# A hybrid attention layer on one core: branch B without normalised rows, output-weight sums by accumulating DMAs, weight scales finished on GpSimd

## The chip, the cores and the metric

The kernel runs on one core of a Trainium2 chip. The metric is the time of one execution on the device, in microseconds (us); smaller is better. The engines are TensorE (PE), VectorE (DVE), ScalarE (ACT), GpSimd (POOL) and SyncE (SP), which here only issues DMAs.

## What is computed

One layer on 512 tokens of width 2048, with 16 learned tokens ahead of them (528 keys). A single input projection feeds two branches. Cut to what matters:

```
proj = rms_norm(h) @ w_in          # q_a, ckv, z_a, indexer q/k/w, q_b, k_b, v_b, z_b, g_a, g_b
# branch A, 8 heads: per query the top keys by an indexer's scores, softmax over them in a latent space
# branch B, 8 heads, queries and keys in two halves of 64:
attn = softmax(q1 k1 * s + bias) - lam * softmax(q2 k2 * s + bias)   # block-causal
o_b  = rms_norm(attn @ v_b, subln_w) * (1 - lam_init)
y_a, y_b = (o_a * silu(z_a)) @ w_o_a, (o_b * silu(z_b)) @ w_o_b
mix  = sigmoid(g_a) * y_a + sigmoid(g_b) * y_b
out  = h + rms_norm(mix @ w_out, post_norm_w)
```

Since o_b is normalised per row, a row of attn may be multiplied by any positive number, as long as the norm's epsilon is multiplied by its square.

## The kernel before

Every float32 factor is taken as a high and a low part of a shorter type, and a product is three passes of TensorE (high x high, high x low, low x high: `mm3`, lines 264 to 267). Weights of `w_in` come in units of 128 columns, two raw tiles of 512 KB each. A unit (class `Unit`) goes through four steps: SP loads its raw tiles (line 179); ScalarE sums the squares of each half (`squares`, line 117); GpSimd takes the maximum over all partitions (`over_rows`, an all-reduce, line 122); VectorE makes a power of two and its inverse from the maximum (`power_of_two`, lines 129 to 135); then ScalarE and VectorE split the raw tile by that scale into `hi` and `lo` (`split16`, lines 161 and 162). The code for a unit's steps stands ahead of the unit's use (`advance`): the loads come three units ahead, squares two, scale and split one. A scheduler then sets the order of all instructions on each engine when the kernel is built, by costs of its own; each engine works its list strictly in order.

The stages, by time: up to 80 us the norms and the first projections; to 186 the indexer's queries and scores; to 560 branch B, head by head; to 745 branch A's heads; to 845 the first gates; to 1230 the other gates in pairs of units (za, zb, then ga and gb; class `Pair`, lines 955 to 990, seven Strassen products per pair, and for zb two multiplications on GpSimd in `load_o`, line 1048); to 1394 the merge stage, 32 units of the two output projections `w_o` (24 products of 512 columns each), their scales made by `wo_bound` and `wo_split`; at last the product with `w_out`, again in seven Strassen products of which four need sums of quarters of `w_out`.

A head of branch B projects q, k and v (48 products each), and meanwhile the head before is attended, in small steps (`step`, `pending`), beside rounds of branch A's top-k (`run_topk`). `b_attend.blk` takes the scores of 128 queries, adds the bias and takes the maximum in one VectorE pass (`softmax`, line 643), combines and negates the maxima (647, 649), lets ScalarE exponentiate (651), then normalises: reciprocal of the two sums, times (1, -lam), one pass over the first probabilities (726) and one that adds the second (727). `pv_steps` transposes the result on TensorE (658). `kstack` writes high and low parts of the two key halves, each to both halves of the partitions (752, 753, 755), so that one product with stacked queries adds high and low.

The sums for `w_out` (`wt_load`, `wt_sums`, lines 250 to 262): 64 tiles of 256 KB are loaded by SP, VectorE subtracts them into 64 tiles, and DMAs from ScalarE's queue store these to `wout_t`; 14 of 16 groups in heads 1 to 7 of branch B, two in the merge stage.

Of the kernel before, what the change touches and what calls it, by code (L numbers as in the profile page):

```python
# [10 lines left out]
F32 = mybir.dt.float32  # L11
# [9 lines left out]
P = 128  # L21
# [47 lines left out]
def layer_kernel(ctx, tc, xt_d, xn_d, cols_d, w0_d, wi_d, wkv_d, wo_d, wout_d, lam_d, post_d,  # L69
# [11 lines left out]
    msq = nc.dram_tensor("o_sumsq", [NH, 512], F32, kind="Internal").ap()  # L81
    rsq = nc.dram_tensor("o_rstd", [NH, 512], F32, kind="Internal").ap()
# [17 lines left out]
    pscale = const.tile([P, 2], F32, name="pscale")  # L100
# [18 lines left out]
    def over_rows(ssq):  # L119

        r = wpool.tile([P, 16], F32, tag="rows", name="rows", bufs=4)[:, :ssq.shape[1]]
        nc.gpsimd.partition_all_reduce(r, ssq, P, bass_isa.ReduceOp.max)  # L122
        return r

    def power_of_two(r, exps):

        e = wpool.tile([P, 2], F32, tag="exp", name="exp", bufs=3)
        if r.shape[1] > 1:
            nc.vector.tensor_reduce(e[:, 0:1], r, AX.X, ALU.max)
            r = e[:, 0:1]  # L130
# [3 lines left out]
        nc.vector.tensor_scalar(sc[:, 0:1], t, -1.0, SFIELD * EXP1, op0=ALU.mult, op1=ALU.add)  # L134
        nc.vector.tensor_scalar(sc[:, 1:2], t, exps, None, op0=ALU.add)
# [110 lines left out]
    wt = {"next": 0, "loaded": []}  # L246

    def wt_load(pool, tags):
        k, n = divmod(wt["next"], 2)
        wt["next"] += 1  # L250
        t = []
        for tag, (ci, di) in zip(tags, ((0, 0), (0, 1), (1, 0), (1, 1))):
            t.append(pool.tile(HB, F32, tag=tag, name="wt"))
            d = nc.sync.dma_start(t[-1], wout_d[ci, di, k, :, 512 * n:512 * n + 512])
            tc.keep_in_program_order(d)
        wt["loaded"].append((k, n, t))
# [251 lines left out]
    nlam = pp.tile([P, 1], F32, name="nlam")  # L508
    nc.vector.tensor_sub(nlam, ldot[:, 1:2], ldot[:, 0:1])
    nc.vector.tensor_scalar(nlam, nlam, -LAM_INIT, None, op0=ALU.add)  # L510
    nc.vector.memset(pscale[:, 0:1], 1.0)
    nc.vector.tensor_copy(pscale[:, 1:2], nlam)
# [106 lines left out]

    PH = ap_.tile([P, 11, P], F32R, name="PH")  # L620
# [35 lines left out]
    def pv_steps(pr, VH, VL, VM, done):  # L656
# [32 lines left out]
        return [tr, pv]  # L689

    def b_attend(h, q, kk, vt):
        q1, q2 = q
        Vn = {}
        pr = p_tiles()
        g = bias_tile(NH + h)
# [759 lines left out]
```

## Time and profile before

| | us |
|---|---|
| median of 3 runs | 1561.2 (1558.08 to 1564.26) |
| the profiled execution: its time | 1558.4 |
| its span in the trace | 1556.6 |
| busy: TensorE | 1443.3 (93%) |
| busy: VectorE | 1161.6 (75%) |
| busy: ScalarE | 982.9 (63%) |
| busy: GpSimd | 150.3 (10%) |
| mean granted clock of TensorE, of 1 | 0.971 |

A busy share is a mean over stages with different limits, so a change is read in the stages that it touches: what the engine that is nearly always busy waits for there. Idle time marked "issue" is time in which an engine waited for nothing that the profile shows.

### The profile page before, as it was taken

What the parts mean: (1) busy time and instruction counts of PE and PEld (TensorE: products, weight loads), DVE (VectorE), ACT (ScalarE), POOL (GpSimd) and SP (SyncE); (2) the same over time, 40 slices, a digit from 0 to 9 for tenths busy, and PEclk for the clock granted to TensorE, in tenths of its full rate; (3) what the DMA queues carried; (4) which work ended last, traced back from release to release, by engine and by line L of the source; (5) the groups of instructions that cost most, each with busy time, mean ns of one, the idle gap of its engine ahead of it and who ended that gap; (6) DMA issues with size and microseconds to landing.
All of it is one profiled execution on the core that took longest, in us unless ns stands there. A gap on an engine that the chain in (4) does not pass through costs nothing. (4 is left out here: it accounts for less than half of the span.)

```text
span 1556.6 us, 25582 instructions
## 1 busy us (share of the span) xinstructions
PE 1443.3 (93%) x9474; PEld 1079.9 (69%) x9474; DVE 1161.6 (75%) x2328; ACT 982.9 (63%) x1749; POOL 150.3 (10%) x203
## 2 busy tenths in 40 slices
PE   7899998898988898999998889999999899999997
PEld 7688766766666666556587768888888544458885
DVE  7975888778888786565677777787778566566778
ACT  7364676656566676666676677777778544436555
POOL 3500000000000022212001100000000011000001
PEclk9899999999999999999999989999999999999999
DMA  6482365445545433122544534444445566446774
GB/s 208 147 272 77 123 203 163 151 141 190 196 140 193 136 116 118 53 96 69 186 155 154 162 116 136 137 141 135 135 144 166 186 211 205 147 167 225 240 248 147
DMA packets 98141, 246.70 MB, mean 158 GB/s; under 512 B 11144, under 2 KB 15432, under 8 KB 97888
## 3 DMA queue, kind: packets, MB, share of 16 engines
q1 hardware_dynamic: 81424, 215.44, 43.5%
q10 hardware_dynamic: 16592, 29.64, 5.1%
q8 instruction: 74, 1.21, 0.3%
q14 instruction: 51, 0.42, 0.1%
HBM read 203.01 MB, written 47.39 MB: 161 GB/s over the span
## 5 line engine op out<-in xcount | busy, mean ns | idle before, releaser
L969 PEld LDWEIGHTS <-wh 128*128 128x128 f16 x2464 | 243.5, 99 | 66.7 <-issue 25.0
L117 ACT ACTIVATE junk<-raw 128x1024 bf16<-128x1024 f32 x192 | 202.1, 1053 | 116.7 <-DMA raw<-in_wi_dram 84.9
L265 PE MATMUL acc<-u,hi 128*128 128x264 f16 (+1 forms) x832 | 267.6, 322 | 1.0 <-DVE kal L783 1.0
L266 PE MATMUL acc<-u,hi 128*128 128x264 f16 (+1 forms) x832 | 267.0, 321 | 0.0
L267 PE MATMUL acc<-u,lo 128*128 128x264 f16 (+1 forms) x832 | 267.0, 321 | 0.0
L969 PE MATMUL acc<-tu,wh 128*128 128x256 f16 x1408 | 237.3, 275 | 20.9 <-DVE r L978 16.1
L969 PE MATMUL acc<-tu,wl 128*128 128x256 f16 x704 | 193.5, 275 | 0.0
L969 PE MATMUL acc<-u,wh 128*128 128x256 f16 x1056 | 180.2, 277 | 9.9 <-ACT wh L161 9.9
L161 ACT ACTIVATE hi<-raw,scale 128x1024 f16<-128x1024 f32 x104 | 118.0, 1143 | 108.2 <-PE acc L266 106.2
L162 DVE SCALAR_TENSOR_TENSOR lo<-raw,scale,hi 128x1024 f16<-128x1024 f32 x104 | 132.9, 1283 | 41.9 <-ACT hi L161 41.2
L265 PEld LDWEIGHTS <-hi 128*128 128x128 f16 x1088 | 108.2, 99 | 79.8 <-issue 6.6
L267 PEld LDWEIGHTS <-lo 128*128 128x128 f16 x1088 | 108.0, 99 | 76.8 <-issue 1.9
L162 DVE SCALAR_TENSOR_TENSOR wl<-S,scale,wh 128x1024 f16<-128x1024 f32 x88 | 115.3, 1311 | 59.8 <-ACT wh L161 59.6
L266 PEld LDWEIGHTS <-hi 128*128 128x128 f16 x1088 | 108.1, 99 | 74.3 <-issue 2.1
L969 PE MATMUL acc<-u,wl 128*128 128x256 f16 x528 | 146.3, 277 | 3.5 <-DVE wl L162 3.5
L122 POOL PARTITION_ALL_REDUCE rows<-ssq x90 | 47.8, 531 | 974.9 <-ACT junk L117 880.6
L969 PEld LDWEIGHTS <-wl 128*128 128x128 f16 x1232 | 121.9, 99 | 20.1 <-DVE wl L162 4.8
L161 ACT ACTIVATE wh<-S,scale 128x1024 f16<-128x1024 f32 x88 | 100.2, 1140 | 33.5 <-DVE S L1076 33.5
L267 PE MATMUL acc<-og,lo 128*128 128x512 f16 x256 | 97.0, 379 | 0.0
L265 PE MATMUL acc<-og,hi 128*128 128x512 f16 x256 | 97.0, 379 | 0.0
L266 PE MATMUL acc<-og,hi 128*128 128x512 f16 x256 | 97.0, 379 | 0.0
L162 DVE SCALAR_TENSOR_TENSOR wl<-raw,scale,wh 128x1024 f16<-128x1024 f32 x66 | 85.4, 1294 | 14.1 <-ACT wh L161 14.0
(309 smaller groups left out, 2978.1 us busy)
## 6 DMA issues: line engine op xcount, KB each, us to landing
raw<-in_wi_dram SPq DMA_DIRECT2D x172, 512.0 KB, 4.3
wt<-in_wout_dram SPq DMA_DIRECT2D x64, 256.0 KB, 4.6
wout_t<-wt ACTq DMA_DIRECT2D x64, 256.0 KB, 3.1
raw<-in_wo_dram SPq DMA_DIRECT2D x32, 512.0 KB, 3.9
raw<-wout_t SPq DMA_DIRECT2D x32, 512.0 KB, 3.9
raw<-in_wout_dram SPq DMA_DIRECT2D x24, 512.0 KB, 4.8
sg<-r ACTq DMA_DIRECT2D x32, 256.0 KB, 3.3
sg<-sg SPq DMA_DIRECT2D x32, 256.0 KB, 3.0
```

The costliest lines, as they stand in the source:

```text
L117: nc.scalar.activation(j, src, AF.Square, accum_out=dst)
L122: nc.gpsimd.partition_all_reduce(r, ssq, P, bass_isa.ReduceOp.max)
L161: nc.scalar.activation(hi, src, AF.Copy, scale=s)
L162: nc.vector.scalar_tensor_tensor(lo, src, s, hi, op0=ALU.mult, op1=ALU.subtract)
L265: nc.tensor.matmul(out, aH, bH, start=start, stop=False)
L266: nc.tensor.matmul(out, aH, bL, start=False, stop=False)
L267: nc.tensor.matmul(out, aL, bH, start=False, stop=stop)
L969: nc.tensor.matmul(acc, a[:, k, :], b, start=first and k == 0 and x == 0, stop=last and x == 2, skip_group_check=True)
```

## The change

It has five parts.

1. Branch B's rows are not normalised: the first exponentials stay as they are, and the second ones are added with the factor -lam z1/z2. The sums z1 are kept in `Z1`, transposed and stored once (`put_sums`), and the norm of o_b adds P * eps * z1 squared in place of eps.
2. Low keys are made once: `kstack` writes one low tile for both halves and copies the high parts to the other half of the partitions by two DMAs of ScalarE's queue. The queries get a third and fourth tile with zeros in the other half (`qstack`, `QZ`), so that a product with the stacked low keys picks its half.
3. The bias pass works with -1 as its factor and takes the minimum of negated logits, the second pass starting from the first's result; lines 647 and 649 go.
4. The sums of `w_out` are made by DMAs that add to their destination, issued by GpSimd (`wt_chain`): 32 loads by SP, 64 accumulating DMAs, 64 stores by SP. The scheduler is no longer told to keep the loads' place. Two of the four sums have the other sign, which `mix_sums` and the second half of `post` take back.
5. A unit's squares are added over its columns by GpSimd ahead of the all-reduce (which then has one column), and the last two steps of `power_of_two` run on GpSimd.

The core of the diff:

```diff
     def over_rows(ssq):
 
-        r = wpool.tile([P, 16], F32, tag="rows", name="rows", bufs=4)[:, :ssq.shape[1]]
-        nc.gpsimd.partition_all_reduce(r, ssq, P, bass_isa.ReduceOp.max)
-        return r
+        r = wpool.tile([P, 8], F32, tag="rows", name="rows", bufs=4)
+        n = ssq.shape[1]
+        while n > 1:
+            n //= 2
+            nc.gpsimd.tensor_tensor(r[:, :n], ssq[:, :n], ssq[:, n:2 * n], ALU.add)
+            ssq = r
+        nc.gpsimd.partition_all_reduce(r[:, 4:5], ssq[:, :1], P, bass_isa.ReduceOp.max)
+        return r[:, 4:5]
 
     def power_of_two(r, exps):
 
         e = wpool.tile([P, 2], F32, tag="exp", name="exp", bufs=3)
-        if r.shape[1] > 1:
-            nc.vector.tensor_reduce(e[:, 0:1], r, AX.X, ALU.max)
-            r = e[:, 0:1]
         t = e[:, 1:2].bitcast(I32)
         nc.vector.tensor_scalar(t, r.bitcast(I32), 24, 23, op0=ALU.logical_shift_right, op1=ALU.logical_shift_left)
         sc = wpool.tile([P, 2], I32, tag="scale", name="scale", bufs=6)
-        nc.vector.tensor_scalar(sc[:, 0:1], t, -1.0, SFIELD * EXP1, op0=ALU.mult, op1=ALU.add)
-        nc.vector.tensor_scalar(sc[:, 1:2], t, exps, None, op0=ALU.add)
+        nc.gpsimd.tensor_scalar(sc[:, 0:1], t, -1.0, SFIELD * EXP1, op0=ALU.mult, op1=ALU.add)
+        nc.gpsimd.tensor_scalar(sc[:, 1:2], t, exps, None, op0=ALU.add)
         f = sc.bitcast(F32)
         return f[:, 0:1], f[:, 1:2]
...
-    def wt_sums():
-        k, n, (b11, b12, b21, b22) = wt["loaded"].pop(0)
-        for i, (o, x, y) in ((0, (b11, b12, b11)), (2, (b12, b22, b12)), (1, (b22, b22, b11)), (3, (b21, b21, b22))):
-            nc.vector.tensor_sub(o, x, y)
-            nc.scalar.dma_start(tscr[i][k, :, 512 * n:512 * n + 512], o)
+    def wt_chain(k, n, tags):
+
+        t = [opool.tile(HB, F32, tag=tag, name="wt") for tag in tags]
+        q = [[wout_d[ci, di, k, :, 512 * n:512 * n + 512] for di in range(2)] for ci in range(2)]
+
+        def put(i, x):
+            nc.sync.dma_start(tscr[i][k, :, 512 * n:512 * n + 512], x)
+
+        def add(x, src):
+            nc.gpsimd.dma_start(x, src, accum_op=ALU.add)
+        nc.sync.dma_start(t[0], q[0][0])
+        nc.sync.dma_start(t[1], q[0][1])
+        yield
+        add(t[0], q[0][1])
+        add(t[1], q[1][1])
+        yield
+        put(0, t[0])
+        put(2, t[1])
+        yield
+        add(t[1], q[0][0])
+        yield
+        put(1, t[1])
+        yield
+        add(t[1], q[1][0])
+        yield
+        put(3, t[1])
+
...
     def softmax(srcs, bias, dst, mx, z):
+
         at = 0
         for i, x in enumerate(srcs):
             n = x.shape[1]
-            nc.vector.tensor_tensor_reduce(dst[:, at:at + n], x, bias[:, at:at + n], 1.0, -3.0e38,
-                                           ALU.add, ALU.max, mx[:, i:i + 1])
+            nc.vector.tensor_tensor_reduce(dst[:, at:at + n], x, bias[:, at:at + n], -1.0,
+                                           mx[:, i - 1:i] if i else 3.0e38, ALU.add, ALU.min, mx[:, i:i + 1])
             at += n
-        if len(srcs) == 2:
-            nc.vector.tensor_scalar(mx[:, :1], mx[:, :1], mx[:, 1:2], -1.0, op0=ALU.max, op1=ALU.mult)
-        else:
-            nc.vector.tensor_scalar(mx[:, :1], mx[:, :1], -1.0, None, op0=ALU.mult)
-        mx = mx[:, :1]
-        nc.scalar.activation(dst, dst, AF.Exp, bias=mx, accum_out=z)
+        nc.scalar.activation(dst, dst, AF.Exp, bias=mx[:, len(srcs) - 1:len(srcs)], scale=-1.0, accum_out=z)
...
-                    mm2(lg[:, :s.stop - s.start], qs, kk[m][0][:, s], kk[m][1][:, s])
+                    nc.tensor.matmul(lg[:, :s.stop - s.start], q[m][:, qs], kk[m][:, s], start=True, stop=False)
+                    nc.tensor.matmul(lg[:, :s.stop - s.start], q[2 + m][:, qs], kk[2][:, s], start=False, stop=True)
                     src.append(lg[:, :n if b < 3 else TH])
-                softmax(src, gb, dst[m], mx[:, 2 * m:2 * m + 2], z[:, m:m + 1])
-            nc.vector.reciprocal(z, z)
-            nc.vector.tensor_mul(z, z, pscale)
-            nc.vector.tensor_scalar(dst[0], dst[0], z[:, 0:1], None, op0=ALU.mult)
+                softmax(src, gb, dst[m], mx[:, 2 * m:2 * m + 2], z[:, 0:1] if m else zs)
+            nc.vector.reciprocal(z[:, 1:2], z[:, 0:1])
+            nc.vector.tensor_scalar(z[:, 1:2], z[:, 1:2], zs, nlam, op0=ALU.mult, op1=ALU.mult)
             nc.vector.scalar_tensor_tensor(dst[0], dst[1], z[:, 1:2], dst[0], op0=ALU.mult, op1=ALU.add)
...
+    def qstack(acc, un, h):
+
+        q = stack64(acc, un, ap_, "q", 4)
+        for m in range(2):
+            hs = slice(64 * m, 64 * m + 64)
+            nc.scalar.activation(QZ[h % 2][m][hs], acc[hs], AF.Copy, scale=un[hs])
+        return list(q) + QZ[h % 2]
+
     def kstack(acc, un):
-        out = [[ap_.tile([P, T], F32R, tag="kk", name=n, bufs=6) for n in ("kh", "kl")] for _ in range(2)]
+
+        kh = [ap_.tile([P, T], F32R, tag="kk", name="kh", bufs=6) for _ in range(2)]
+        kl = ap_.tile([P, T], F32R, tag="kk", name="kl", bufs=6)
         for t in range(2):
             s = slice(TH * t, TH * t + TH)
-            for m, (kh, kl) in enumerate(out):
-                hs, os_ = slice(64 * m, 64 * m + 64), slice(64 - 64 * m, 128 - 64 * m)
-                nc.scalar.activation(kh[hs, s], acc[t][hs, :TH], AF.Copy, scale=un[hs])
-                nc.scalar.activation(kh[os_, s], acc[t][hs, :TH], AF.Copy, scale=un[hs])
-                for d in (hs, os_):
-                    nc.vector.scalar_tensor_tensor(kl[d, s], acc[t][hs, :TH], un[hs], f32(kh[hs, s]),
-                                                   op0=ALU.mult, op1=ALU.subtract)
-        return out
+            for m in range(2):
+                hs = slice(64 * m, 64 * m + 64)
+                nc.scalar.activation(kh[m][hs, s], acc[t][hs, :TH], AF.Copy, scale=un[hs])
+                nc.vector.scalar_tensor_tensor(kl[hs, s], acc[t][hs, :TH], un[hs], f32(kh[m][hs, s]),
+                                               op0=ALU.mult, op1=ALU.subtract)
+        for m in range(2):
+            hs, os_ = slice(64 * m, 64 * m + 64), slice(64 - 64 * m, 128 - 64 * m)
+            nc.scalar.dma_start(f32(kh[m][os_]), f32(kh[m][hs]))
+        return kh + [kl]
...
     for h in range(NH):
+        for i in range(2):
+            wt_now.append(wt_chain(h, i, [f"o{6 + 4 * (h % 2) + 2 * i + x}" for x in range(2)]))
...
```

What moves on the engines shows at three places, in the order of instructions as built.

GpSimd's list in branch B, before (`ssq` are a unit's sums of squares, `rows` the all-reduce's result, `G` a bias tile); the line is that of the program:

```order
L122 ISA rows_3254<-ssq_2952 128x2
L122 ISA rows_3423<-ssq_3164 128x2
L636 MEMSET G_3893 64x64
L122 ISA rows_3589<-ssq_3355 128x2
L122 ISA rows_3809<-ssq_3507 128x2
L122 ISA rows_3981<-ssq_3719 128x2
L636 MEMSET G_4451 64x64
L122 ISA rows_4147<-ssq_3909 128x2
L122 ISA rows_4367<-ssq_4065 128x2
L122 ISA rows_4538<-ssq_4277 128x2
```

The same place after the change; a row "ISA" with nothing behind it is an instruction without operands that the compiler puts in:

```order
L128 ISA
L128 ISA rows_4288<-rows_4288 128x1
L137 ISA
L137 TENSOR_SCALAR scale_4381<-exp_4379 128x1
L138 TENSOR_SCALAR scale_4381<-exp_4379,uexp_85 128x1
L126 TENSOR_TENSOR rows_4468<-ssq_4196 128x1
L128 ISA
L128 ISA rows_4468<-rows_4468 128x1
L653 MEMSET G_4905 64x64
L137 ISA
L137 TENSOR_SCALAR scale_4528<-exp_4526 128x1
L138 TENSOR_SCALAR scale_4528<-exp_4526,uexp_85 128x1
```

Before, branch B's list holds all-reduces and memsets alone. Now two scale steps stand behind each all-reduce and an addition ahead of it, and bare ISA rows stand between the two kinds, 45 in branch B where there were none.

GpSimd's list in the merge stage, before (one row for each unit of `w_o`, 32 in all):

```order
L122 ISA rows_14525<-ssq_14471 128x1
L122 ISA rows_14581<-ssq_14513 128x1
L122 ISA rows_14623<-ssq_14569 128x1
L122 ISA rows_14671<-ssq_14611 128x1
L122 ISA rows_14713<-ssq_14659 128x1
```

After the change (`ogscale` holds the exponents of the attention's output):

```order
L128 ISA
L128 ISA rows_14324<-ssq_14264 128x1
L128 ISA rows_14366<-ssq_14312 128x1
L128 ISA rows_14414<-ssq_14354 128x1
L137 ISA
L137 TENSOR_SCALAR scale_14357<-exp_14355 128x1
L138 TENSOR_SCALAR scale_14357<-exp_14355,ogscale0_12992 128x1
L137 TENSOR_SCALAR scale_14405<-exp_14403 128x1
L138 TENSOR_SCALAR scale_14405<-exp_14403,ogscale1_13005 128x1
L137 TENSOR_SCALAR scale_14447<-exp_14445 128x1
L138 TENSOR_SCALAR scale_14447<-exp_14445,ogscale0_12992 128x1
L128 ISA
```

Two or three all-reduces stand together, then their scale steps; 29 bare rows stand among the 32 units where there were none.

SP's list from the last raw tiles of the indexer (line 144, after the change 147) to the first units of the heads (179, after 182), before:

```order
L144 DMA raw<-in_wi_dram 128x1024
L572 DMA bias_rows<-bias_by_distance 128x656 x2
L144 DMA raw<-in_wi_dram 128x1024 x4
L179 DMA raw<-in_wi_dram 128x1024 x4
L144 DMA raw<-in_wi_dram 128x1024
L179 DMA raw<-in_wi_dram 128x1024 x6
L635 DMA G<-bias_rows 128x528 x2
```

After the change (259 and 260 load tiles of `w_out`, 255 stores a sum):

```order
L259 DMA wt<-in_wout_dram 128x512
L260 DMA wt<-in_wout_dram 128x512
L259 DMA wt<-in_wout_dram 128x512
L182 DMA raw<-in_wi_dram 128x1024
L255 DMA wout_t<-wt 128x512 x2
L260 DMA wt<-in_wout_dram 128x512
L255 DMA wout_t<-wt 128x512 x3
L259 DMA wt<-in_wout_dram 128x512
L255 DMA wout_t<-wt 128x512
L260 DMA wt<-in_wout_dram 128x512
L259 DMA wt<-in_wout_dram 128x512 x2
L182 DMA raw<-in_wi_dram 128x1024
```

Before, no tile of `w_out` is loaded until head 1. Now its loads and the stores of sums stand between the raw loads of the first units; each store waits for an accumulating DMA that GpSimd issues. In GpSimd's list 27 of the 64 accumulating DMAs stand ahead of the first unit's all-reduce.

## Rows read from the trace of the kernel before

**Rows 1.** Stages: us, busy us of PE, PEld, DVE, ACT, POOL; PEclk, DMA share, GB/s
```profile
186.00:560.00 374.00, 333.86 (x2338) 249.56 (x2337) 311.41 (x912) 240.25 (x468) 19.26 (x38) 0.95 0.51 167
...
930.00:1190.00 260.00, 250.08 (x2255) 221.40 (x2255) 204.98 (x259) 192.91 (x288) 6.57 (x16) 0.99 0.43 139
...
1230.00:1394.00 164.00, 164.00 (x761) 75.47 (x759) 102.66 (x206) 68.11 (x95) 14.65 (x26) 1.00 0.53 168
```

**Rows 2.** Waits of PE, longest in total: us, times, longest us
```profile
PE acc L658 <- DVE pr L727: 30.9, 8, 6.1
...
PE acc L969 <- DVE r L978: 16.1, 14, 5.2
```

**Rows 3.** Lines of DVE in branch B, 186 to 560: busy us, mean ns | idle before
```profile
L261 DVE TENSOR_TENSOR wt<-wt 128x512 f32<-128x512 f32 x56 | 37.1, 684 | 0.6 <-DMA wt<-in_wout_dram 0.4
...
L755 DVE SCALAR_TENSOR_TENSOR kl<-acc,scale,kh 64x264 fp32r<-64x264 f32 x64 | 31.4, 491 | 16.2 <-ACT kh L753 14.8
...
L726 DVE TENSOR_SCALAR pr<-pr,z 128x144 f32<-128x144 f32 (+3 forms) x31 | 11.9, 384 | 0.2
...
L649 DVE TENSOR_SCALAR mx<-mx 128x1 f32<-128x1 f32 x48 | 6.7, 142 | 0.0
...
L135 DVE TENSOR_SCALAR scale<-exp,uexp 128x1 int32<-128x1 int32 x27 | 5.4, 203 | 0.0
...
L134 DVE TENSOR_SCALAR scale<-exp 128x1 int32<-128x1 int32 x27 | 4.0, 148 | 0.3
...
L129 DVE TENSOR_REDUCE exp<-rows 128x1 f32<-128x2 f32 x27 | 3.8, 149 | 20.6 <-POOL rows L122 20.6
```

**Rows 4.** Timeline of POOL in branch A: start, us [idle before <- releaser]
```profile
629.62 0.37 POOL L122 PARTITION_ALL_REDUCE rows<-ssq  x1 [6.37 <-issue]
...
637.38 4.31 POOL L817 TENSOR_TENSOR gm<-G,sc 128x528 f32<-128x528 f32 x3 [7.39 <-issue]
...
653.10 0.37 POOL L122 PARTITION_ALL_REDUCE rows<-ssq  x1 [6.10 <-ACT PH L670]
```

**Rows 5.** Timeline in branch B: a unit's all-reduce, and the split that uses it
```profile
287.52 0.35 POOL L122 PARTITION_ALL_REDUCE rows<-ssq  x1 [12.65 <-ACT junk L117]
...
320.69 1.15 ACT L161 ACTIVATE hi<-raw,scale 128x1024 f16<-128x1024 f32 x1 [1.24 <-PE acc L266]
```

**Rows 6.** Waits of DVE for all-reduces, whole span: us, times, longest us
```profile
DVE exp L129 <- POOL rows L122: 52.1, 26, 6.8
```

**Rows 7.** Timeline of SP: raw loads of the first units
```profile
128.81 21.92 SPq L179 DMA_DIRECT2D raw<-in_wi_dram  x4
```

**Rows 8.** DMA issues of the page: count, KB each, median us to landing
```profile
raw<-in_wi_dram SPq DMA_DIRECT2D x172, 512.0 KB, 4.3
...
wt<-in_wout_dram SPq DMA_DIRECT2D x64, 256.0 KB, 4.6
...
wout_t<-wt ACTq DMA_DIRECT2D x64, 256.0 KB, 3.1
```

**Rows 9.** Timeline at a zb pair's start: POOL's all-reduce, and PE's product
```profile
829.84 0.39 POOL L122 PARTITION_ALL_REDUCE rows<-ssq  x1 [6.13 <-issue]
...
832.03 0.39 PE L969 MATMUL acc<-u,wh 128*128 128x256 f16 x2 [2.80 <-ACT wh L161]
```

**Rows 10.** Timeline of a later pair: all-reduce, first split, a split's low half, product
```profile
986.53 0.42 POOL L122 PARTITION_ALL_REDUCE rows<-ssq  x1 [18.50 <-ACT junk L117]
...
995.67 1.13 ACT L161 ACTIVATE wh<-raw,scale 128x1024 f16<-128x1024 f32 x1
...
998.26 1.27 DVE L162 SCALAR_TENSOR_TENSOR wl<-raw,scale,wh 128x1024 f16<-128x1024 f32 x1
...
1003.57 0.27 PE L969 MATMUL acc<-u,wh 128*128 128x256 f16 x1
```

**Rows 11.** Timeline in the merge stage: a unit's all-reduce, and its split
```profile
1248.12 0.82 POOL L122 PARTITION_ALL_REDUCE rows<-ssq  x1 [3.42 <-ACT junk L117]
...
1261.38 1.15 ACT L161 ACTIVATE hi<-raw,scale 128x1024 f16<-128x1024 f32 x1 [2.70 <-PE acc L266]
```

More of the change, by code (lines that the diff above doesn't have):

```diff
@@ L244, in weights, with wt_step @@
         return hi, lo
[L246 to L256, printed above, removed]
-    def wt_sums():
-        k, n, (b11, b12, b21, b22) = wt["loaded"].pop(0)
-        for i, (o, x, y) in ((0, (b11, b12, b11)), (2, (b12, b22, b12)), (1, (b22, b22, b11)), (3, (b21, b21, b22))):
-            nc.vector.tensor_sub(o, x, y)
-            nc.scalar.dma_start(tscr[i][k, :, 512 * n:512 * n + 512], o)
+    def wt_chain(k, n, tags):
[21 more added lines that the diff above has]
+        put(3, t[1])
+    wt_now = []
+    def wt_step():
+        for g in list(wt_now):
+            if next(g, "end") == "end":
+                wt_now.remove(g)
     def mm3(out, aH, aL, bH, bL, start, stop):
@@ L618, in run_topk @@
             f()
+    Z1 = ap_.tile([P, NH * NB], F32, name="Z1")
     PH = ap_.tile([P, 11, P], F32R, name="PH")
@@ L691, in b_attend @@
     def b_attend(h, q, kk, vt):
-        q1, q2 = q
         Vn = {}
@@ L762, in small_weights @@
         for i, n in enumerate(("wuk", "wuv")):
-            raw = ap_.tile([P, 2, 256], F32, tag="raw2", name="raw2", bufs=2)
+            raw = opool.tile([P, 2, 256], F32, tag=f"o{14 + i}", name="raw2")
             nc.sync.dma_start(raw, wkv_d[j, :, i])
@@ L857, in layer_kernel @@
             small_weights(0)
-        for i in range(2 if h else 0):
-            wt_sums()
         for acc, un in proj_kv("vb", h):
             step()
-            run_topk(TK.pop(0))
+            between()
         vt = ap_.tile([P, T], F32, tag="vt", name="vt", bufs=1)
@@ L892, in layer_kernel, with put_sums @@
     run_topk(1000)
+    def put_sums():
+        pt = psum()
+        nc.tensor.transpose(pt[:NH * NB, :P], Z1, ident)
+        zt = ap_.tile([NH * NB, P], F32, name="zt")
+        nc.scalar.copy(zt, pt[:NH * NB, :P])
+        nc.sync.dma_start(zscr.rearrange("h (b p) -> (h b) p", p=P), zt)
     for h in range(NH):
@@ L1034, in wide @@
         return zp.tile(HB, F32, tag="r", name=nm, bufs=bufs)
-    rv = zp.tile([P, 32], F32, name="rv")
+    rv, zv = [zp.tile([P, 32], F32, name=n) for n in ("rv", "zv")]
     nc.sync.dma_start(rv, msq.rearrange("h (a b) -> (h a) b", b=32))
-    rstd_cols(rv, rv, P)
+    nc.sync.dma_start(zv, zscr.rearrange("h (a b) -> (h a) b", b=32))
+    nc.vector.tensor_mul(zv, zv, zv)
+    nc.vector.scalar_tensor_tensor(rv, zv, P * EPS, rv, op0=ALU.mult, op1=ALU.add)
+    nc.scalar.activation(rv, rv, AF.Sqrt, scale=1.0 / P)
+    nc.vector.reciprocal(rv, rv)
     nc.sync.dma_start(rsq.rearrange("h (a b) -> (h a) b", b=32), rv)
@@ L1247, in layer_kernel @@
             sgs.append(load_sg(c + 2))
-        if c in (3, 6):
-            wt_load(yp, [f"w{x}" for x in range(4)])
         for ab in range(2):
```

38 lines of the change are left out of this document (22 added, 16 removed).

## The prediction

> **What bounds the kernel now.** I read the table of stages first [rows 1]. TensorE is the engine that is nearly always busy: 333.86 of 374 us in branch B (186 to 560), 250.08 of 260 in the later pairs (930 to 1190), 164.00 of 164 in the merge stage (1230 to 1394). VectorE comes second, at 311.41 of 374 us in branch B (83%) and 204.98 of 260 in the pairs (79%). GpSimd works 19.26 us in all of branch B. Then the list of waits says what TensorE waits for [rows 2]: its longest entry, 30.9 us in eight waits, is branch B's own, the transposes of line 658 behind the last combination of a head's probabilities (line 727). The next entry belongs to the pairs. So VectorE is what holds TensorE up in branch B, and the lines of VectorE [rows 3] say what the change takes from there. Last I looked at what one GpSimd instruction costs when it follows one of another kind [rows 4], because the change puts such neighbours everywhere; this decides my forecast.
>
> **Branch B, what VectorE loses.** Per head, from [rows 3]: four normalisations at 384 ns (1.5 us), four of eight low-key products at 491 ns (2.0), the 56 subtractions for the output weights at 684 ns over seven heads (5.5), the maxima of line 649 at 142 ns and their like of line 647 (about 1.2), and three units' reductions and two scale steps (3 x (149 + 148 + 203) ns, 1.5). That is about 11.7 us of the 39 that a head has. ScalarE gives up four copies of keys and takes two of queries and two DMA issues, which I call even. What this can be worth is bounded by what it removes: nothing at the least, at most the 30.9 us of [rows 2] and 17 us of clock (the stage's granted clock is 0.95 of full speed, a mean over its two levels of 1.2 and 2.4 GHz, and 333.86 us of TensorE work at full clock would be 0.05 x 333.86 shorter). The waits of 3 to 6 us go first, so I take -31.
>
> **Branch B, what GpSimd gains.** The three scale steps of a unit stay a chain, but two of its links move to GpSimd, and one or two additions come ahead of the all-reduce. The trace shows the price of such neighbours, without a name: in branch A an all-reduce starts at 629.62 and takes 0.37, and the tensor operations behind it begin at 637.38, after 7.39 us in which they wait for nothing that is shown ("issue"); the next all-reduce, at 653.10, starts 6.10 us after GpSimd's work before it ended [rows 4]. I call it a switch: 7.4 us from all-reduce to ordinary operations, 6.1 us back, 13.5 us for the round trip. The order of instructions has a bare ISA row at each switch; branch B has none now, though memsets stand between its all-reduces, so a memset needs none. In the changed kernel there are 45 bare rows there, 22.5 round trips. Each also holds an all-reduce (0.37) and the moved operations, which the trace has nowhere on GpSimd; between 0.15 us (VectorE's own steps [rows 3]) and 1.44 (a third of 4.31, a wide product [rows 4]) I take 0.2 each, 0.6 in all, nearest to VectorE's because they are of one column. So GpSimd has 22.5 x 14.5 = 326 us of work, beside the 374 - 31 = 343 us that the stage would then take. It fits with 17 us to spare, and a scale has time: the all-reduce at 287.52 serves the split at 320.69 [rows 5]. But VectorE takes its links in order, and its wait for an all-reduce (52.1 us in 26 times now, up to 6.8 [rows 6]) grows by up to 6.1 us in each of 24 units. I take +26 of those 146 us, so branch B nets -5; its ends are -48 (relief and clock, the switches hidden) and +60 (91 of the 146 us not hidden).
>
> The Trainium skill, GPSIMD Engine Reference, section 2.1, tells of an unseen load of about 6 us, measured at 5.95, at the first call of code newly put on that engine, and it speaks against this change. The trace agrees in kind and is dearer in one direction; with 5.95 us both ways a round trip would be 11.9 us, and the merge stage's term below would be some 23 us smaller.
>
> **The output weights' sums.** 64 accumulating DMAs go to GpSimd's queue, 64 stores to SP's, and the order pulls all of them forward, in between the raw loads that SP issues in order from 128.81 on, four in 21.92 us [rows 7]. A chain is one load (4.6), three additions and three stores (3.1 each) in series [rows 8]. No row shows an accumulating DMA; it is bounded by a store of the same size, 3.1, and three times a load, 13.8. I take 4.6, the load it is nearest to: 4.6 + 13.8 + 9.3 = 27.7 us a chain, four in flight, sixteen in all, so 111 us between about 75 and 190. The raw loads queue behind; later in the branch they are early by more than the 33 us of [rows 5], in front by less, and I take +10, between 0 and +40 (additions at three times the load make each chain 55 us). GpSimd's issues hold its queue as well, at a price that no row has; 18 of the 64 remain in branch B, where a microsecond each would use up the spare 17.
>
> By the Trainium skill, DMA: Bandwidth & Descriptors, Anatomy of one DMA, GpSimd's path takes 2.0 us and the bytes over 436e3 a microsecond: an estimate of 2.6 us for 256 KB. By it a chain would be 21.7 us and this term 0; no run here shows it yet.
>
> **Branch A**: a round trip for each head is there already [rows 4], and there are 17 bare rows before and after: 0, between -3 and +10.
>
> **za, zb and the first pairs (745 to 930).** Here an all-reduce already comes at the end of a switch (idle 6.13 us, "issue") and TensorE stands 2.80 us behind the split that it releases [rows 9]. The change puts a 7.4 us switch between that all-reduce and that split. Four pairs have no slack (30 us); the other three or four have some, and I put 15 on them: +45, between +15 (the multiplications of line 1048 no longer need a switch of their own) and +80.
>
> **Later pairs (930 to 1190).** There are no switches now, and one round trip a pair in the new order. From the all-reduce at 986.53 the split follows at 995.67 and the product that needs it at 1003.57, 17.0 us later [rows 10]. The new chain is 0.4 + 6.1 + 0.4 + 0.2 + 7.4 + 0.4, then the split's halves (1.13 and 1.27): 17.3 us. It is late by 0.3 us, and while it runs VectorE, with about 4 us free in a pair of 19, stands up to 6.1. I take 1 us for each of 13 pairs, +13, between 0 and +45.
>
> **Merge stage.** Nothing waits now: the all-reduce of 1248.12 serves a split at 1261.38 [rows 11], TensorE takes 164.00 us for 32 units, 5.1 us each. The new order has 29 bare rows: 14.5 round trips for 32 units. GpSimd then needs 14.5 x 13.5 = 196 us, and 32 x 0.8 = 25 for the all-reduces and scales, 221 us; about one trip lies ahead of 1230. That is 207 against 164: +43, and +5 for the gates' own scales at 1190. This term needs no view of slack, since GpSimd simply cannot supply more; its ends are +25 and +85 (units that wait for raw tiles, since a tile is free only after its split). The subtractions that leave this stage, the sign changes, the half of the post weights on GpSimd, the two loads of rv and zv: 0, beside TensorE's work in both stages.
>
> **Sum.** -5 + 10 + 0 + 45 + 13 + 48 = +111 us on the profiled execution's 1558.4 us (span 1556.6), 1669; the median of the runs is 1561.2, 0.2% above. I forecast **1670 us**. The ends add to -11 and +320.
>
> **The rivals.**
> *The relief decides.* If a switch's load can run ahead of the wait that it follows, so that a round trip costs under 164 / 14.5 = 11.3 us with all its operations, the merge stage keeps TensorE's pace, the pairs' lead of 17 us covers the chain, and branch B keeps its -31 to -48. With +10 left at 830 that is about 1530. For it: leads of 33 us in branch B [rows 5]. Against: the two directions were paid in full each time that they occur in these rows, and an all-reduce that TensorE was waiting for stood behind one [rows 4, 9]. The point is that 11.3 us.
> *The sums hold the front up.* If an accumulating DMA costs three loads, or keeps GpSimd itself for some microseconds, SP's raw loads come late from 130 to 260 and GpSimd's first all-reduces too: +40 for the loads instead of +10, and 64 x 1 us of GpSimd, half of it in time that it has: about 1730. For it: 27 accumulations precede the first unit's all-reduce in the new order. Against: they are spread over 100 us.
> The Trainium skill, SBUF - State Buffer, Who interferes with whom, says that VectorE's two-port operations lock GpSimd out while it writes a DMA's descriptors; it would make this rival more likely, and no run here shows it.
> *GpSimd sets the pace everywhere.* If each of the 24 units in branch B also waits a further 2 to 3 us between its links, GpSimd needs 24 x 17 = 408 us there, 13 pairs take 2.3 us more each, and the terms are +34 in branch B (not -5), +30 in the pairs (not +13) and +85 in the merge stage (not +43): about 1767, with more beyond it.
> *Nothing in sum*: the lowest ends, -11 us, and up to 15 more: 1550 to 1566.
>
> **How the numbers follow.** The forecast 0.55, the sums 0.16, GpSimd everywhere 0.14, the relief 0.10, nothing in sum 0.05. The range leaves out the relief, nothing in sum and what of the pace set by GpSimd lies far out (0.05): 1585 to 1790. A measurement of this kernel can tell about 0.5% from no change, 8 us. Faster by more than that 0.10, within it 0.05, slower 0.85.
>
> **What would show it.** Right: some 70 switches on GpSimd of 6 to 7.5 us each, a merge stage of some 200 us in which TensorE waits for splits and these for GpSimd's scales; TensorE waiting behind the splits of 830 to 905 for about 10 us each; waits of line 658 nearly gone. Wrong: ordinary operations that follow an all-reduce at once, a merge stage of 164 us with TensorE always busy, or raw loads that leave SP 40 us late at 150.

## The result and the profile after

The changed kernel takes 1750.67 us (median of 4 runs, 1749.79 to 1760.22) against 1559.64 us for the kernel before on the same chip: a ratio of 1.1235, 95% interval 1.1187 to 1.1283. It is slower by 191 us where I had forecast 111. The profiled execution has a span of 1749.0 us at a mean granted clock of 0.928 of full speed (a mean over the two levels, 1.2 and 2.4 GHz; 0.971 before).

Where the time went is read by landmarks that both traces have: the first product of head 1 of branch B, the first of branch A, the last projection ahead of the pairs (so a wait at the first pair's start counts with the pairs), the start of the eighth pair, the first product of the merge stage and the first with `w_out`. In the kernel before, the pairs start at 773 us by this measure, and the merge stage at 1215. The table gives the length of each stretch before, and how much longer it is in each run (the runs with names are told of below; the last column is up to the last product).

```
us               front  heads   branch  za, zb, later  merge  last    all
                 to B1  B1-B7   A       first  pairs   stage  product
before           209.3  344.7   218.9   153.8  288.4   175.4  155.3
the change       +77.8  -10.9    +9.7   +37.7  +41.7   +37.1   -0.6  +192.4
e1_scales_dve    +81.8  -13.5    +0.8    +0.6   +2.0    +0.7   -0.0   +72.4
e2_sums_dve      +17.2   +4.7    +2.4   +42.8  +41.3   +41.2   -0.5  +149.1
e3_both_back      +0.7   -6.1    +0.5    +5.3   +2.0    +0.6   -0.5    +2.6
e4_scales_only   +11.6   -4.4   +14.4   +40.2  +40.2   +41.1   -0.5  +142.4
e6_pinned        +16.8  +58.3    +1.1    -0.3   -0.2    +1.6   -0.5   +76.8
e7_put_pool      +85.3  -13.0    -0.1    +1.3   +2.4    +0.1   -0.5   +75.6
e8_plain         +55.9  -18.9    +1.0    +0.3   +1.3    +2.2   -0.6   +41.2
e9_adds_only     +10.9   -4.4    +0.2   +16.2   +9.5    +0.9   -0.6   +32.7
e10_pin_all       +8.2  +11.4    +0.3    +4.7   +2.3    +0.0   -0.6   +26.2
e11_free_stores  +81.9  -27.4    +0.1    +3.6   +0.1    -0.1   -0.3   +58.0
e12_no_subs       +1.3  -23.7    +2.1    +0.7   +1.6    +1.6   -0.4   -16.7
e13_spread_sums   +5.8  -13.4    +5.9    +1.6   +2.6    +0.2   -0.4    +2.2
```

The top of the list of TensorE's waits after the change (engine, line, waited for: us in total, times, longest) answers to [rows 2]:

```profile
PE acc L1011 <- ACT wh L164: 67.5, 25, 7.6
PE lg L545 <- ACT relu L566: 40.3, 4, 26.5
PE acc L284 <- ACT hi L164: 26.4, 10, 8.6
PE acc L671 <- DVE pr L740: 22.2, 6, 6.7
PE s L734 <- DMA kh<-kh: 19.3, 2, 17.9
```

The old first entry, the transposes behind the last combination, is down from 30.9 to 22.2. Ahead of it stand splits (line 164) in pairs and merge stage, 67.5 and 26.4 us, and in the front four waits for one ScalarE pass, 40.3 us. The last row is new work: the first head's key copy by DMA, which ScalarE issued after 11.45 us of standing for a raw tile. What the splits wait for shows in the list of GpSimd's waits:

```profile
POOL rows L128 <- issue: 400.4, 63, 8.0
POOL scale L137 <- issue: 230.4, 31, 9.1
```

And in VectorE's, where the row answers to [rows 6]:

```profile
DVE exp L135 <- POOL rows L128: 113.6, 61, 9.0
```

The switches are there as read from [rows 4]: 400.4 / 63 = 6.4 us ahead of an all-reduce, 230.4 / 31 = 7.4 us ahead of a scale step. VectorE's waits for all-reduces grew from 52.1 to 113.6 us. GpSimd's timeline in the merge stage (start, us, [idle before <- releaser]) shows two round trips of 15 us, two units each:

```profile
1450.69 0.82 POOL L128 PARTITION_ALL_REDUCE rows<-ssq  x2 [5.95 <-issue]
1458.55 0.18 POOL L137 TENSOR_SCALAR scale<-exp 128x1 int32<-128x1 int32 x1 [7.03 <-DVE sg L1306]
...
1465.54 0.93 POOL L128 PARTITION_ALL_REDUCE rows<-ssq  x2 [6.09 <-ACT m L1285]
1474.49 0.18 POOL L137 TENSOR_SCALAR scale<-exp 128x1 int32<-128x1 int32 x1 [8.02 <-DVE sg L1306]
```

TensorE's 10.3 us of products for two units cannot fill 15. Its timeline has the wait just behind that second scale:

```profile
1475.91 0.61 PE L284 MATMUL acc<-og,hi 128*128 128x512 f16 x1 [2.79 <-ACT hi L164]
```

The stage as a whole, from its first product to its last, in the view of stages (columns as in [rows 1]), before:

```profile
1215.25:1390.70 175.45, 170.28 (x794) 78.39 (x792) 103.37 (x217) 72.59 (x103) 15.71 (x29) 0.98 0.54 173
```

And after the change:

```profile
1371.20:1583.70 212.50, 183.26 (x793) 79.30 (x792) 93.13 (x151) 73.78 (x106) 27.91 (x90) 0.93 0.38 121
```

It is 37 us longer: TensorE is idle for 29 us where it was for 5, and it has 13 more us of work for the same products, because its granted clock, 0.98 before, is 0.93 now. (The row of [rows 1] from 1230 to 1394 leaves out the first 15 us of the stage.) The row at 1475.91 shows the clock after a wait: a product of 0.61 us, 0.38 at full speed.

The front is another thing. The stages of 30 us ahead of branch B, after the change:

```profile
100.00:130.00 30.00, 30.00 (x149) 24.71 (x148) 24.42 (x39) 15.48 (x31) 4.40 (x5) 1.00 1.02 314
130.00:160.00 30.00, 9.70 (x48) 7.75 (x47) 4.61 (x7) 3.60 (x7) 7.72 (x9) 0.74 1.01 258
```

The DMA engines' share (last but one) is 1.0 from 100 to 160, and from 130 to 160 TensorE works 9.70 us of 30. In the same place the kernel before has:

```profile
130.00:160.00 30.00, 29.96 (x143) 24.11 (x143) 17.74 (x35) 17.50 (x34) 0.93 (x3) 1.00 0.26 79
```

ScalarE's list says what hangs on it, from 60 to 300 us: a unit's squares wait 29 us for a raw tile, and the indexer's pass that TensorE needs stands behind them.

```profile
ACT junk L118 <- DMA raw<-in_wi_dram: 66.5, 9, 29.0
```

That raw tile is the first of the heads' units. SP's timeline and ScalarE's have its load and the squares that waited for it:

```profile
156.36 1.22 SPq L182 DMA_DIRECT2D raw<-in_wi_dram  x1
...
163.61 1.06 ACT L118 ACTIVATE junk<-raw 128x1024 bf16<-128x1024 f32 x1 [29.03 <-DMA raw<-in_wi_dram]
```

Before, it left SP at 128.81 [rows 7]. So it comes late mainly because it leaves SP 27.5 us later, and only some 3 us because it takes longer to land (7 us here, 3.8 at the median before). The fourth of these loads leaves at 191.72, 41 us late. What SP stood for, from 60 to 300 us, is its own list of waits: stores of sums, behind additions that had not landed.

```profile
SPq L255 <- DMA wt<-in_wout_dram: 110.7, 35, 10.3
```

### The profile page after: what moved, and what is told of

Its sections match the earlier page's. It is cut to its first block, busy times and chain, and to the rows that moved or that the text cites. A ratio compares the mean times of both kernels' runs of the same rounds, so it can differ in the third digit from the quotient of the medians.

```text
span 1749.0 us, 25693 instructions
## 1 busy us (share of the span) xinstructions
PE 1492.9 (85%) x9475; PEld 1094.1 (63%) x9475; DVE 1070.9 (61%) x1858; ACT 984.3 (56%) x1734; POOL 298.7 (17%) x544
## 3 DMA queue, kind: packets, MB, share of 16 engines
q0 software_dynamic: 9216, 16.78, 5.7%
HBM read 211.42 MB, written 47.41 MB: 148 GB/s over the span
## 4 chain that ended last, share of the span: by engine, by line
PE 39%; DMA 16%; issue 14%; DVE 12%; ACT 11%; POOL 3%; SPq 0%; POOLq 0%; ACTq 0%; DVEq 0%
PE acc L1011 10%; DMA raw<-in_wi_dram 6%; PE acc L284 6%; PE acc L285 6%; PE acc L286 6%; DMA wt<-in_wout_dram 4%; ACT junk L118 3%; PE acc L1403 3%; PE acc L1405 3%; PE acc L1404 3%; ACT wh L164 2%; DVE lo L165 2%; DMA wout_t<-wt 2%; ACT hi L164 2%; DVE wl L165 2%
## 5 line engine op out<-in xcount | busy, mean ns | idle before, releaser
L1011 PEld LDWEIGHTS <-wh 128*128 128x128 f16 x2464 | 249.7, 102 | 124.9 <-ACT wh L164 76.3
L1011 PE MATMUL acc<-u,wh 128*128 128x256 f16 x1056 | 203.2, 298 | 63.8 <-ACT wh L164 63.8
L1011 PE MATMUL acc<-u,wl 128*128 128x256 f16 x528 | 157.1, 298 | 6.1 <-DVE wl L165 6.1
L1011 PEld LDWEIGHTS <-wl 128*128 128x128 f16 x1232 | 125.6, 102 | 29.1 <-DVE wl L165 9.2
L284 PE MATMUL acc<-og,hi 128*128 128x512 f16 x256 | 101.9, 398 | 24.7 <-ACT hi L164 24.7
L285 PE MATMUL acc<-og,hi 128*128 128x512 f16 x256 | 101.3, 396 | 0.0
L164 ACT ACTIVATE wh<-raw,scale 128x1024 f16<-128x1024 f32 x66 | 75.3, 1142 | 45.8 <-POOL scale L137 43.4
```

Of the source, the lines that this page charges most:

```text
L164: nc.scalar.activation(hi, src, AF.Copy, scale=s)
L284: nc.tensor.matmul(out, aH, bH, start=start, stop=False)
L285: nc.tensor.matmul(out, aH, bL, start=False, stop=False)
L1011: nc.tensor.matmul(acc, a[:, k, :], b, start=first and k == 0 and x == 0, stop=last and x == 2, skip_group_check=True)
```

## The experiments

Theory A was the prediction's: switches on GpSimd cost what is lost behind head 1, the sums' DMAs what is lost before it, by the queues of SP and GpSimd. The letters that follow name its rivals, each told where it is expected.

**e1_scales_dve.** `over_rows` and `power_of_two` as before, the rest of the change kept:

```diff
-        nc.gpsimd.tensor_scalar(sc[:, 0:1], t, -1.0, SFIELD * EXP1, op0=ALU.mult, op1=ALU.add)
+        nc.vector.tensor_scalar(sc[:, 0:1], t, -1.0, SFIELD * EXP1, op0=ALU.mult, op1=ALU.add)
...
```

> The change with part 5 undone: the columns' maximum and the last two scale steps are back on VectorE, GpSimd has all-reduces and accumulating DMAs. Theory A (GpSimd's switches cost what is lost behind head 1 of branch B, the sums' queue what is lost before it): the stretch up to head 1 stays about 78 us later than before, the 127 us lost after branch B (branch A 10, first gates 34, later pairs 46, merge 37) go: about 1620 us, branch B some 10 us shorter still. Rival B (the accumulating DMAs slow the whole): it stays above 1700.

Measured: 1637.47 us (ratio to before 1.0486, 1.0436 to 1.0536). Behind branch B all but some 4 us of the loss are gone; the front keeps its own. The median is 17 us above the 1620 expected. Theory A's division holds; rival B falls.

**e2_sums_dve.** The reverse: `wt_load` and `wt_sums` back, with the signs of `mix_sums` and `post`.

```diff
-            wt_now.append(wt_chain(h, i, [f"o{6 + 4 * (h % 2) + 2 * i + x}" for x in range(2)]))
+            wt_load(opool, [f"o{6 + 4 * ((h + i) % 2) + x}" for x in range(4)])
...
```

> The change with part 4 undone: the sums of the output weights are back on VectorE with their loads in heads 1 to 7, scales stay on GpSimd. Theory A: the 78 us before head 1 go, the rest stays: about 1675 us. Rival C (the late first all-reduces on GpSimd, with their switches, hold the front): 50 us or more of the 78 stay, about 1725 us.

Measured: 1706.61 us (1.0896, 1.0851 to 1.0942). Of the front's 78 us 61 go, as A says; but the heads are 16 us longer than in the change, with VectorE's subtractions back in them (e12 shows what these cost): 1707, not 1675. The 17 us that stay in the front are near the 12 that part 5 alone costs there (e4 in the table), so the switches are not free in the front.

**e3_both_back.** Parts 1 to 3 alone (both edits above).

> Parts 4 and 5 undone, parts 1 to 3 alone (no normalised rows, low keys once, negated maxima). Theory A: branch B's relief without cover: 10 to 40 us faster than before, 1520 to 1550 us. Rival D (the relief is worth nothing, the transposes wait for something else then): 1555 to 1565 us.

Measured: 1561.74 us, ratio 0.9997 (0.9972 to 1.0023): rival D's figure. Branch B gains 6 us, and 5 of them go again in the first pairs. So the relief that I had priced at 31 us is not worth that by itself; e12 asks why.

**e4_scales_only.** Part 5 alone on the kernel before.

> Part 5 alone on the kernel before. Theory A: 127 us lost behind branch B and some in it, where VectorE waits longer for all-reduces: 1685 to 1720 us. Rival E (the switches only cost where the sums have put GpSimd late already): below 1600 us.

Measured: 1700.40 us (1.0877, 1.0836 to 1.0919), with the change's own losses behind branch B to within 5 us a stretch. Part 5 costs 138 us alone (against 1562.67 us for the kernel before in the same round) and 113 beside the rest (the change against e1). Rival E falls.

**e6_pinned.** e1, with each chain's first loads held at their place in the program's order on SP:

```diff
-        nc.sync.dma_start(t[0], q[0][0])
-        nc.sync.dma_start(t[1], q[0][1])
+        for x in range(2):
+            tc.keep_in_program_order(nc.sync.dma_start(t[x], q[0][x]))
```

> Parts 1 to 4 with the scales on VectorE, and each chain's two first loads kept at their place in the program's order on SP, so that no chain starts before its head. Theory A (the sums hold the front up because their stores stand among the raw loads of the indexer and the first heads): the stretch up to head 1 of branch B comes within 15 us of before (it is 82 us late without the pin), and the heads keep the 43 us of the run with the scales on VectorE: about 1540 us, 1525 to 1560. Rival B (accumulating DMAs are dear wherever they stand): branch B's heads lose what the front gains, above 1600 us.

Measured: 1635.68 us (1.0474, 1.0426 to 1.0522), no better than e1. The loss moved: the front is 17 us late, and heads 1 to 7 are 58 us longer: the first three by 70, the others shorter by 12. The scheduler packed the chains into the heads up to the fourth (additions from 184 to 457 us). There SP's own list of waits, from 310 to 380, shows its queue held by stores that wait for additions:

```profile
SPq L253 <- DMA wt<-in_wout_dram: 55.4, 14, 8.1
```

**e7_put_pool.** e1, with the stores on GpSimd's queue (`nc.sync` to `nc.gpsimd` in `put`).

> Parts 1 to 4 with the scales on VectorE, no pin, but the 64 stores of the sums go out on GpSimd's queue, behind the additions that they wait for; SP keeps only the 32 loads. Theory A (SP's in-order queue): raw loads leave SP in time and the front (head 1 of branch B at 291 us, 82 late) loses less than 40 us: below 1600 us. Rival F (the bytes: some 42 MB more on the DMA engines between 75 and 260 us): the front stays 60 us or more late, 1620 us or more.

Measured: 1634.40 us (one run), head 1 85 us late: rival F's outcome. But the edit did not free SP. A chain's first load now stands in SP's list until the stores that GpSimd issues have left its tiles free; SP's waits from 60 to 300 us:

```profile
SPq L257 <- DMA wout_t<-wt: 66.2, 10, 14.7
SPq L258 <- DMA wout_t<-wt: 59.4, 10, 18.3
```

That is 126 us of 240, where SP stood 130.1 for additions in e1, so the run doesn't tell theory A from rival F.

**e8_plain.** e1, with copies in place of additions (`accum_op` left out, and with it the sums).

> Parts 1 to 4 with the scales on VectorE, no pin, and GpSimd's 64 DMAs copy instead of adding: the sums of the output weights are left out, the order and the bytes stay nearly as they are. Rival G (the addition itself is the price, 6.9 us to landing at the median): the front's loss halves, below 1600 us. Theory A (the serial chain in SP's queue): each link is only some 2 us shorter, the front gains 10 to 25 us of 82: 1610 to 1630 us.

Measured: 1601.17 us (one run), head 1 56 us late. The copies are worth 31 us in all in the traces, 26 of them in the front: more than A gave them and less than half of the loss, so neither expectation was met. A chain is quicker, too: sixteen of them, four in flight, last from 71 to 285 us here and from 70 to 319 in e1. The profile page's rows of DMA queues (packets, MB, share of 16 engines' span) show one reason. The change's:

```profile
q0 software_dynamic: 9216, 16.78, 5.7%
```

And e8's:

```profile
q0 software_dynamic: 5120, 16.78, 3.0%
```

The same 16.78 MB take 5.7% of 1749.0 us as additions, 100 us of all 16 engines, and 3.0% of 1599.4 us, 48 us, as copies. The other runs whose row holds the 64 additions alone have 95 to 106 us, e10 with its spread chains the most.

**e11_free_stores.** e1, with stores that depend on no addition (the sums are left out):

```diff
-            nc.sync.dma_start(tscr[i][k, :, 512 * n:512 * n + 512], x)
+            nc.sync.dma_start(tscr[i][k, :, 512 * n:512 * n + 512], q[i // 2][i % 2])
```

> Parts 1 to 4 with the scales on VectorE, no pin; the 64 stores copy from the output weights themselves instead of the sums (which are left out), so that none waits for an addition, while the number of DMAs and their bytes stay. Theory A (waits in the queues): head 1 of branch B less than 40 us late instead of 82, below 1600 us. Rival F (the DMA engines are full between 80 and 310 us): head 1 stays 60 us or more late, 1615 us or more.

Measured: 1616.26 us (one run), head 1 still 82 us late. Its stages of 30 us, to be held against the two of the change:

```profile
100.00:130.00 30.00, 29.87 (x147) 24.23 (x146) 26.19 (x43) 18.18 (x36) 1.97 (x3) 1.00 1.02 326
130.00:160.00 30.00, 12.81 (x62) 10.26 (x60) 5.84 (x10) 3.88 (x8) 12.97 (x16) 0.77 1.01 237
```

No store waits for an addition here, and the loss is the same while the DMA engines are full (share 1.02 and 1.01): rival F's outcome. But theory A does not fall by it. The next chain's loads (lines 257 and 258) need tiles that additions still write, and they hold SP's list instead of the stores. SP's waits from 60 to 300 us:

```profile
SPq L258 <- DMA wt<-in_wout_dram: 47.8, 9, 13.9
SPq L257 <- DMA wt<-in_wout_dram: 28.9, 9, 8.5
```

And the first raw load of the heads' units leaves SP later still, in SP's timeline:

```profile
170.30 0.53 SPq L180 DMA_DIRECT2D raw<-in_wi_dram  x1
```

The stores now read memory as well (228.19 MB read in all, 211.42 in e1), so the bytes did not stay the same either. In every run that loses 50 us or more in the front, raw loads leave SP late and the DMA engines are full or nearly so from 130 to 160 (share 0.85 in e8, 1.0 or more in the others). How much of SP's standing comes from the full engines, and how much from the order of its list, no run separates.

**e10_pin_all.** e1, with loads, additions and stores of the chains all held in the program's order, so that they lie evenly over 8 heads:

```diff
+            tc.keep_in_program_order(nc.gpsimd.dma_start(x, src, accum_op=ALU.add))
...
```

> Parts 1 to 4 with the scales on VectorE, and every DMA of the chains (loads, additions, stores) kept at its place in the program's order: two chains a head, one step in each half of a projection, so additions and the stores behind them stand some 7 us apart, and the chains are spread over 8 heads instead of 4. Theory A (SP and GpSimd stand in their queues for additions that were scheduled as if they landed at once): the front and the heads lose nothing and the heads take 43 us: 1530 to 1550 us. Rival F (an accumulating DMA takes twice the time of the DMA engines that a plain one does, and this total is what is paid wherever it lies): 1590 us or more.

Measured: 1579.20 us (1.0105, 1.0077 to 1.0133): between the two. Against e3, which has the sums on VectorE, the chains cost 1579.2 - 1561.7 = 17 us when spread and 1637.5 - 1561.7 = 76 when packed, so most of the price was their place. But the heads are 11 us longer than before and not 13 shorter as in e1. Two stages of 80 us in the heads show a DMA share (last but one) of 0.79 and 0.76, and TensorE idle for 3 and 10 us; why the heads do not gain there was not taken further.

```profile
320.00:400.00 80.00, 76.75 (x544) 56.63 (x543) 50.47 (x142) 48.62 (x95) 14.15 (x20) 0.98 0.79 206
400.00:480.00 80.00, 70.31 (x462) 50.35 (x461) 57.36 (x156) 46.86 (x93) 14.17 (x21) 0.91 0.76 200
```

**e9_adds_only.** The kernel before, with the additions of squares alone on GpSimd.

> The kernel before with only the additions of the squares on GpSimd, ahead of the all-reduce; the scale steps stay on VectorE. Theory A (any ordinary operation beside an all-reduce costs the two switches): the way back is off the chain (6.4 us before the all-reduce, none behind it), but GpSimd still pays 13.8 us a round trip; the merge stage has no additions there (one column), so its 41 us go and about half of the pairs' 47: 1590 to 1630 us. Rival H (the moved scale steps themselves are what costs): within 15 us of before.

Measured: 1591.11 us (one run), +32.7 in the trace: the merge stage, where a unit has one column and nothing to add, loses 0.9 us and not 41; the gates and later pairs lose 26 and not 80. A switch ahead of the all-reduce costs too, though its operation is off the chain behind it; the larger part is the switch between all-reduce and split. Rival H falls, as the time lies 15 us beyond its range.

**e12_no_subs.** e3, with the 64 subtractions left out and their DMAs kept:

```diff
-            nc.vector.tensor_sub(o, x, y)
             nc.scalar.dma_start(tscr[i][k, :, 512 * n:512 * n + 512], o)
```

> Parts 1 to 3 alone (1561.7 us, no gain), with the 64 subtractions for the output weights left out on VectorE, their loads and stores kept, so that the sums are left out. Theory J (VectorE's relief pays only once the subtractions are gone too, since they stand ahead of a head's last combination): heads of 43 us instead of 47 and 1535 us, 1525 to 1545. Rival K (the wait at a head's end is a chain of scores, exponentials and combination that no relief shortens): 1555 us or more, and the heads of 43 us in the runs without VectorE's sums come from the fewer DMAs there.

Measured: 1541.53 us (one run), the heads 24 us shorter than before and 18 shorter than in e3: theory J. TensorE's waits for the combination, from 164 to 532, against 27.4 us in e3 and 30.9 in [rows 2]:

```profile
PE acc L652 <- DVE pr L721: 14.8, 7, 3.3
```

**e13_spread_sums.** e3, with the groups of sums moved to where VectorE has time.

```diff
-        for i in range(2 if h else 0):
-            wt_load(opool, [f"o{6 + 4 * ((h + i) % 2) + x}" for x in range(4)])
+        if 1 <= h <= 5:
+            wt_load(opool, [f"o{6 + 4 * (h % 2) + x}" for x in range(4)])
...
```

> Parts 1 to 3, scales and sums on VectorE as in the kernel before, but the 16 groups of sums spread over stages in which VectorE has time: 3 loaded beside the indexer's last queries, 5 in heads 1 to 5 of branch B (they were 14 in heads 1 to 7), 4 in branch A's first four heads, 4 in the merge stage (they were 2). Theory J (branch B's relief pays as the subtractions leave it: 22 us with all 14 groups gone): 9 of 14 groups gone and the places where they go hide them: 8 to 16 us faster than parts 1 to 3 alone, 1546 to 1554 us. Rival L (they cost in their new places what they gave): 1558 to 1566 us.

Measured: 1560.41 us, ratio 0.9989 (0.9967 to 1.0012): rival L. The heads gain 13.4 us as J says, the front and branch A give back 11.7. No version tried that keeps the sums beats the kernel before.

## Why the prediction was right, and where it was not

The direction and the mechanism with the largest part hold; the size was short by 80 us, and the front's term failed.

- *A round trip on GpSimd costs 13.5 us.* Shown: 6.4 + 7.4 in the waits after the change; e1 takes them away and 113 us with them, e4 adds them alone and 138 us. The Trainium skill's figure in GPSIMD Engine Reference, section 2.1, about 6 us for a first call to newly loaded code, is near the way to the all-reduce; here it is paid each time, and the way to the scale steps is 7.4, so the measured ones decide.
- *Merge stage 207 us, +43 and +5.* 212.5 us from its first product to its last (175.4 + 37.1). Right in kind. The loss is smaller than 43 because the 164 us taken off were the stage without its first 15 us and their wait. I had not said that part of it is clock: of the 37 us, 24 are waits and 13 slower products (183.26 us of work, 170.28 before).
- *za, zb and the first pairs, +45.* +37.7. Right in kind: TensorE stands behind a split once in each pair, at 857, 880 and 957 us for 6.92, 4.50 and 4.27 us. The eight waits up to 1035 are of 3.6 to 6.9 us, not of about 10. The chain is the one of [rows 9] with the switch in it, in the timeline of GpSimd and TensorE:

```profile
947.23 0.38 POOL L128 PARTITION_ALL_REDUCE rows<-rows  x1 [6.26 <-issue]
...
955.16 0.18 POOL L137 TENSOR_SCALAR scale<-exp 128x1 int32<-128x1 int32 x1 [7.55 <-issue]
...
956.58 0.61 PE L1011 MATMUL acc<-u,wh 128*128 128x256 f16 x2 [4.27 <-ACT wh L164]
```

- *Later pairs, +13.* +41.7, near the end of its bounds: the term was mis-sized. The steady pairs are as reckoned, about 1 us each (8 us from the eighth to the sixteenth). The other 34 us fall in the last seven. Two of these, from 1252 to 1311, take 20 of them: there the gates' own scales, which I had at +5, put two more round trips in front of a pair's. The other 14 us were not taken further. The timeline of GpSimd from 1265 to 1304, and the product that waits:

```profile
1265.10 0.38 POOL L128 PARTITION_ALL_REDUCE rows<-rows  x1 [7.64 <-issue]
...
1279.06 1.82 POOL L128 PARTITION_ALL_REDUCE rows<-rows  x2 [5.82 <-issue]
...
1295.58 0.38 POOL L128 PARTITION_ALL_REDUCE rows<-rows  x1 [6.18 <-issue]
1303.53 0.18 POOL L137 TENSOR_SCALAR scale<-exp 128x1 int32<-128x1 int32 x1 [7.57 <-issue]
...
1304.95 0.61 PE L1011 MATMUL acc<-u,wh 128*128 128x256 f16 x2 [7.62 <-ACT wh L164]
```

- *Branch A, 0.* +9.7, at the end of its bounds; e4 has 14.4. A likely reason, not tested by itself: I counted bare rows alike before and after, but the scale steps now stand behind the switch that only branch A's own products had stood behind.
- *Branch B, -5.* -10.9 in heads 1 to 7. Right as a sum, and not as its parts: the waits of line 658 are not nearly gone (22.2 us of 30.9 are left), and the relief of 31 us is not parts 1 to 3's. e3 gives 6 and e12, with the subtractions gone too, 24, so most of what pays is the departure of the subtractions. Whether it would pay without parts 1 to 3 was not tried and stays open.
- *The sums, +10 with an end at +40.* **This is the step that failed**: "I take 4.6, the load it is nearest to: 4.6 + 13.8 + 9.3 = 27.7 us a chain". It took an addition's latency from loads of branch B, where the DMA engines' share is 0.51 [rows 1], and a chain as the bare sum of its links. For such a stage 4.6 was right: the 18 additions that leave after 250 us land in 4.4 us at the median. The 46 ahead of them, packed between 77 and 247 us where the bias rows and raw tiles are, take 8.2, with the DMA engines' share at 0.8 or more from 80 to 260; the time that an addition takes of these engines (100 us of all 16 for the 64, copies 48) was in no term. And each link stands in SP's or GpSimd's list behind the links of other chains: in e1, without switches, sixteen chains last from 70 to 319 us, 62 us each with four in flight (an estimate), above even the 55 of the far end.

  So the raw loads do queue behind, as said, but by 27 to 47 us for the first units (the fourth leaves 41 us late at 150, which I had named as a sign of being wrong), and the front is 77.8 us late. e10 shows that spreading the chains takes away some 60 of 76 us. Whether the full engines or the lists' order weigh more stays open, since neither e7 nor e11 freed SP. The second rival named the place and the way and gave 1730, nearer than my 1670. The Trainium skill, DMA: Bandwidth & Descriptors, Anatomy of one DMA, by which I had estimated 2.6 us, would have made the term 0; no addition of the change landed in less than 3.9 us, and the measured ones decide.

The forecast's missing 80 us are thus the front (68), the later pairs (29) and branch A (10), less what the gates, the merge stage with its +5, and the heads came out lower (25).

## What to carry to other kernels

Count the places where GpSimd changes between an all-reduce and ordinary operations, stage by stage, and charge both directions (6.4 and 7.4 us here) against the period of that stage; moving a unit's small steps, of one or two columns each, to an idle engine cost 113 to 138 us. Before DMAs are added, add their time on the DMA engines (for an accumulating one, twice a copy's) to the share of the stage in which a scheduler will put them, and ask what stands behind them in the issuing engine's list. Then read where that engine stands: an edit that frees a list of one wait can put another in its place, as e7 and e11 did. Work taken from a busy engine pays only where it stands ahead of what the bounding engine waits for: three parts of this change freed VectorE and brought nothing by themselves; with the subtractions gone too the time fell by 20 us.

## What was not expected of the hardware

An accumulating DMA of 256 KB takes the DMA engines twice as long as a copy issued in the same way (100 against 48 us for 16.78 MB), in 9216 packets instead of 5120. One issue holds GpSimd for 0.86 us at the least and 1.04 at the median of the change; the row at 122.48 has one that waited for a store that left SP late:

```profile
122.48 0.86 POOL L258 DMA_DIRECT2D wt<-in_wout_dram  x1 [26.43 <-DMA wout_t<-wt]
```

And an addition of one or two columns on GpSimd, mostly of 0.18 to 0.35 us, took 1.05 to 1.3 us at fifteen places of the change; why was not tried. One of two columns:

```profile
1252.42 1.17 POOL L126 TENSOR_TENSOR rows<-ssq 128x2 f32<-128x2 f32 x1 [5.27 <-ACT junk L118]
```
